# Reordered weight sums, late rows and bank products in the feed-forward part of an attention block

## The chip, the cores and the metric

The kernel runs on one core of a Trainium2 chip. A core has five engines with a queue each: TensorE (PE in the profile, its weight loads PEld) multiplies into PSUM banks of 128 x 512 float32; VectorE (DVE), ScalarE (ACT) and GpSimd (POOL) work element by element; SyncE (SP) only issues transfers here. They wait for one another through semaphores. The metric is the device time in microseconds; lower is better.

## The reference

One layer of an encoder on x of 2048 rows by 1024 columns, in float32. Two kinds of attention come first, then the part this change is about:

```python
h = h + jnp.einsum('bse,ed->bsd', mix, w_out[l])
u2 = rms_norm(h, norm2_w[l])
gate = jnp.einsum('bsd,df->bsf', u2, w_gate[l])
up = jnp.einsum('bsd,df->bsf', u2, w_up[l])
h = h + jnp.einsum('bsf,fd->bsd', jax.nn.silu(gate) * up, w_down[l])
```

The inner width is 2816.

## The kernel before

The attention stages run up to about 1380 us and are untouched by the change. The feed-forward part then works through 22 steps: two halves of 1024 rows, and in each half 11 groups of 256 inner columns. The steps are numbered i = 0 to 21.

**Precision and products.** TensorE multiplies in float16. Each float32 operand is split in a high and a low float16 part, and a product is the sum of three matmuls (high x high, low x high, high x low). Every 2 x 2 block product is done with seven block products in place of eight (Winograd's form of Strassen's scheme), so operands exist as seven combinations `o`.

**A step.** `gate` and `up` each call `quad`, which issues seven products of 12 matmuls each (`product`, L1004), 84 matmuls in all, and adds the parts up on VectorE. The banks are named `pa`, `pm` and `pd`: `pa` and `pd` each take two products, the second added on top of the first after another engine has read the first (L1014 reads `pa`, L1031 reads `pd`). The order of the products in `quad` is pa, pm, pm, pa again, pd, pm, pd again. A finished block goes to a callback `c11`: for gate a SiLU on ScalarE (L1049), for up the multiplication with the gate (L1069) and the split of the result into the buffer `act` (L1063, L98), of which there are two. `down` (L1104) multiplies `act` by the down weight, for two steps at once: for the first half it runs in steps 2, 4, 6, 8 and 10, and in step 11 for the one group left over, each time between gate and up. Its partial sums are read from and written back to the DRAM buffer `hd` through four tiles `hs`. In step 11 the first half's result goes out. In the second half the odd tiles of `hs` use the weight buffers `stages`, which are then idle.

**Loading weights.** In the first half each step's gate, up and down weight is loaded as float32 by `load_ffn`: a transfer into one of two buffers `stages` (L909, L911), a Square on ScalarE (`sq`, L937 for gate and up, L189 for down), a sum or maximum across the partitions with a few matmuls into the bank `fsc` (L945 for gate and up, L182 in `across` for down), a scale worked out by six short VectorE instructions, and then the split into float16 parts on ScalarE, GpSimd and VectorE (L215, L98, L220) and a store of them to the DRAM buffer `split`. The second half reads `split` and does none of this. `load_ffn` is a generator: `begin` runs it through the load and the Square, `end` runs the rest. `quad` calls a hook after its fourth product: in gate `begin` for the next step's gate weight; in up `end` for this step's down weight and then `begin` for the next step's up weight. The other calls stand between the quads.

**Late rows.** The last four of the 16 row tiles get their second norm, transposes and seven combinations inside steps 0 and 1 (`build_x`, another generator, moved on by `tick`; transposes on TensorE at L1178). It occupies one of the two `act` buffers and all four `hs` tiles until it ends. It yields 14 times. Before the change it is moved on in bunches: one step in the gate quad of step 0, three after it, three in the up quad, one after, and all the rest after the gate quad of step 1.

**The order of the work.** The program is traced in the order written, and a scheduler then orders each engine's queue at build time: it plays the program through with estimated durations, and an engine takes, of the instructions that are ready by that estimate, the one traced first. So an instruction can be issued ahead of ones traced before it, and in the built program each queue is fixed. Such an order can be bound by an edge, `tc.issue_after(ins)`: what is traced in its block on `ins`'s engine is queued behind `ins`, without waiting for its end. The kernel before has one, for a transfer.

Of the kernel before, what the change touches and what calls it, by code (L numbers as in the profile page):

```python
# [21 lines left out]
S, D, P = 2048, 1024, 128  # L22
# [18 lines left out]
CU = 3  # L41
# [18 lines left out]
def block(tc, a, out):  # L60
# [3 lines left out]
    with top:  # L64
# [113 lines left out]

        def across(dst, pt, cols):
            k = len(cols)  # L180
            for j, c in enumerate(cols):
                PE.matmul(pt[:, P * j : P * j + P], lhsT=c.to_broadcast([P, P]), rhs=id32[:], start=True, stop=True)  # L182
            DVE.tensor_reduce(dst, pt[:, : P * k], op=ALU.max, axis=AX.X)
# [689 lines left out]
        with ExitStack() as ph2:  # L873
# [20 lines left out]

            rows = []
            stages = fw.tile([P, 2, 2048], F32, name="stages", bufs=1)
            turn = [0]
# [22 lines left out]
            def load_ffn(half, fg, names, W):  # L920
                eng = "ADP" if fg == 0 else WE
                sc = scales.setdefault(fg, {})
                for nme in names:
# [19 lines left out]
                    def columns(m):  # L943
                        for k in range(KT):
                            PE.matmul(pt[:, :256], lhsT=ones[:], rhs=sq[:, 256 * k : 256 * k + 256], start=k == 0, stop=k == KT - 1)  # L945
# [54 lines left out]
            def product(ps_, wv, wo, X, xo, start, stop):  # L1000
                q = 0
                for kt in range(4):
                    for xi, wi in ((0, 0), (1, 0), (0, 1)):
                        PE.matmul(ps_[:].rearrange("p (t n) -> p t n", n=P), lhsT=wv[:, wo, wi, 128 * kt : 128 * kt + 128], rhs=X[xo][:, :, xi, kt, :], start=start and q == 0, stop=stop and q == 11, skip_group_check=not start)  # L1004
                        q += 1

            def quad(wv, X, tag, bufs, c11, hook=None):
                def cst():
                    return fp.tile([P, 512], F32, tag=tag, bufs=bufs, name=nm(tag))

                pa = pst("pa")
                product(pa, wv, 0, X, 0, True, True)
                u2 = cst()
                ACT.copy(u2[:], pa[:])  # L1014
# [16 lines left out]
                DVE.tensor_tensor(c22[:], pd[:], u3[:], ALU.add)  # L1031
# [6 lines left out]
                DVE.tensor_tensor(u2[:], u2[:], pd[:], ALU.add)  # L1038
                c11(0, 1, u2)

            def gate(W, X, hook=None):
                sg = {}

                def on_gate(f, t, c):
                    if (f, t) == (0, 0):
                        s = fp.tile([P, 512], F32, tag="cg", bufs=5, name=nm("cg"))
                    else:
                        s = c
                    ACT.activation(s[:], c[:], AF.Silu, scale=W["kg"][:])  # L1049
                    sg[f, t] = s  # L1050

                quad(W["g"], X, "cg", 5, on_gate, hook)
                note("A", 2000)
                return sg

            def up(W, X, sg, hook=None, final=False):
                if final:
# [25 lines left out]

                quad(W["u"], X, "cu", CU, on_up, hook)
# [12 lines left out]
            def down(half, units, hs, last, hook=None):  # L1097
# [3 lines left out]
                def prod(po, ao, wo, j, start=True):  # L1101
                    for u, (W, act) in enumerate(units):
                        for q, (xi, wi) in enumerate(((0, 0), (0, 1), (1, 0))):
                            PE.matmul(po[:], lhsT=act[:, ao, xi, 128 * j : 128 * j + 128], rhs=W["d"][:, wo, wi, :], start=start and u == 0 and q == 0, stop=u == nu - 1 and q == 2, skip_group_check=not start)  # L1104

# [12 lines left out]
                for j in range(4):  # L1118
                    if j == 2 and hook is not None:
                        hook()  # L1120
                    if j + 1 < 4:
                        hs.append(load_hs(half, j + 1, nu == 3))
                    h0, h1 = hs[j]
# [31 lines left out]
            def build_x():  # L1155
# [11 lines left out]
                for j in (2, 3):  # L1167
# [6 lines left out]
                    for z in (xa, xb):  # L1174
                        for h in range(2):
                            tr = pst("xtr")
                            for k in range(4):
                                PE.transpose(tr[:, P * k : P * k + P], z[:, 512 * h + P * k : 512 * h + P * k + P], id32[:])  # L1178
                            ACT.copy(z[:, 512 * h : 512 * h + 512], tr[:])
                        note("A", 1000)  # L1180
# [3 lines left out]
            W = {}  # L1184
# [35 lines left out]
            for i, (half, fg) in enumerate(steps):  # L1220
# [77 lines left out]
```

## Time and profile before

| | |
|---|---|
| median of 3 runs | 2701.52 us (2700.67 to 2704.35) |
| the profiled execution | 2702.93 us |
| its span | 2701.0 us |
| TensorE busy | 2508.6 us, 93% |
| VectorE busy | 1959.8 us, 73% |
| GpSimd busy | 1517.8 us, 56% |
| ScalarE busy | 1344.7 us, 50% |

In the profile, L1004 is line 1004 of the kernel. A row of a group reads: line, engine, operation, output<-inputs by the program's tile names with buffer numbers left out, shape, count. In the timeline a row starts with its start and its length in us, and ends with the idle time of the engine before it and what ended that. A helper's line stands for all its callers: L98 is any addition or subtraction, L220 any low part of a weight. A tile's name is that of the last user of a buffer, so `pm<-X,wg` can be another of the quad's products. The granted clock is the share of full speed that TensorE was given.

### The profile page before, as it was taken

To read this page: it belongs to the slowest core of one execution; us is meant where nothing else is said; L and a number is where in the kernel's file an instruction comes from. 1 tells how busy PE (TensorE), PEld (TensorE's weight loads), DVE (VectorE), ACT (ScalarE), POOL (GpSimd) and SP (SyncE) were. 2 spreads that over 40 slices of the span, in tenths; PEclk is the share of its full clock that TensorE was granted. 3 is DMA by queue.
4 is the path that set the end of the run, shared out by engine and by line. 5 is a ranking of instruction groups with operands and counts; after the bars stand their busy time and mean duration, and the time that the engine had idled before them with its cause. 6 is when DMAs were issued, how large, how long until landed. Compare 5 with 4: busy or idle time off the path is not lost. (4 is left out here: it accounts for less than half of the span.)

```text
span 2701.0 us, 50505 instructions
## 1 busy us (share of the span) xinstructions
PE 2508.6 (93%) x19628; PEld 1507.6 (56%) x19628; DVE 1959.8 (73%) x3712; ACT 1344.7 (50%) x2487; POOL 1517.8 (56%) x1097
## 2 busy tenths in 40 slices
PE   7998989899988989889999999999999999999999
PEld 4655656577776776567774444444444444444444
DVE  6898879899989889887866877778685543433434
ACT  4665656567978878765634534435352112111121
POOL 2578767768767767545665755665564332322323
PEclk9999999999999999999999999999999999999999
DMA  6778697768989989997996566565748744635532
GB/s 221 211 163 184 143 200 172 172 145 183 195 175 185 178 166 206 208 205 203 230 317 232 211 232 219 207 239 183 253 171 330 304 159 157 234 132 184 202 110 94
DMA packets 619584, 534.40 MB, mean 198 GB/s; under 512 B 480640, under 2 KB 548224, under 8 KB 609104
## 3 DMA queue, kind: packets, MB, share of 16 engines
q1 hardware_dynamic: 617520, 529.09, 70.1%
q8 instruction: 154, 2.52, 0.4%
q0 software_dynamic: 512, 1.36, 0.2%
q14 instruction: 86, 0.70, 0.1%
q10 hardware_dynamic: 1312, 0.72, 0.1%
HBM read 261.08 MB, written 147.32 MB: 151 GB/s over the span
## 5 line engine op out<-in xcount | busy, mean ns | idle before, releaser
L98 POOL TENSOR_TENSOR s<-z,s 128x1024 f16<-128x1024 f32 (+7 forms) x288 | 471.5, 1646 | 141.8 <-ACT s L89 118.2
L506 PE MATMUL sc<-kT,qT 128*128 128x512 f16 (+3 forms) x1520 | 382.7, 354 | 51.1 <-DVE z L622 18.6
L1104 PE MATMUL pd<-wd,act 128*128 128x512 f16 x1764 | 392.8, 380 | 5.3 <-DVE cu L1038 4.7
L621 DVE TENSOR_TENSOR_SCAN z<-z,sc 128x512 f32<-128x512 f32 (+3 forms) x320 | 352.8, 1112 | 56.5 <-ACT sc L619 34.6
L325 PE MATMUL pj<-w,xt 128*128 128x384 f16 x1920 | 354.6, 333 | 17.1 <-ACT raw L374 5.8
L1004 PEld LDWEIGHTS <-wu 128*128 128x128 f16 x1848 | 181.9, 98 | 224.6 <-issue 12.8
L1004 PEld LDWEIGHTS <-wg 128*128 128x128 f16 x1848 | 181.3, 98 | 222.9 <-issue 9.3
L517 PE MATMUL yp<-v,aT 128*128 128x64 f16 (+1 forms) x4896 | 271.2, 205 | 36.9 <-DMA aT<-s 35.7
L517 PEld LDWEIGHTS <-aT 128*128 128x128 f16 x4896 | 239.1, 100 | 114.4 <-DMA aT<-s 46.7
L98 POOL TENSOR_TENSOR act<-cg,act 128x512 f16<-128x512 f32 x109 | 150.7, 1393 | 259.4 <-ACT act L1063 259.4
L1104 PEld LDWEIGHTS <-act 128*128 128x128 f16 x1764 | 172.9, 98 | 213.5 <-issue 7.2
L325 PEld LDWEIGHTS <-xt 128*128 128x128 f16 x1920 | 187.8, 99 | 147.2 <-issue 23.4
L89 ACT CAST s<-z 128x128 f16<-128x128 f32 (+7 forms) x215 | 173.3, 810 | 135.9 <-DMA aT<-s 44.6
L98 POOL TENSOR_TENSOR stages<-stages 128x512 f32<-128x512 f32 x97 | 171.4, 1767 | 116.5 <-DVE wg L220 42.2
L618 ACT ACTIVATE z<-sc,c 128x512 f32<-128x512 f32 (+3 forms) x320 | 211.2, 665 | 24.4 <-PE sc L506 12.4
L98 POOL TENSOR_TENSOR hs<-hs,cu 128x512 f32<-128x512 f32 x102 | 133.6, 1317 | 159.3 <-DVE hs L1110 59.7
L506 PEld LDWEIGHTS <-qT 128*128 128x128 f16 x1520 | 128.8, 99 | 119.7 <-issue 23.9
L831 PE MATMUL po<-wo,mt 128*128 128x256 f16 x1536 | 182.4, 279 | 12.6 <-DVE xf L834 8.6
L1063 ACT CAST act<-cg 128x512 f16<-128x512 f32 x126 | 76.7, 616 | 231.1 <-DVE cg L1069 192.7
L1110 DVE SCALAR_TENSOR_TENSOR hs<-pd,c,hs 128x512 f32<-128x512 f32 x144 | 106.0, 747 | 115.0 <-PE pd L1104 105.3
L341 PE MATMUL pj<-xt,w 128*128 128x128 f16 x2304 | 177.4, 222 | 6.2 <-DVE v L363 5.2
L1004 PE MATMUL pm<-X,wu 128*128 128x512 f16 x792 | 179.8, 381 | 2.1 <-ACT cg L1049 1.7
(254 smaller groups left out, 4812.3 us busy)
## 6 DMA issues: line engine op xcount, KB each, us to landing
xt<-xs SPq DMA_DIRECT2D x112, 512.0 KB, 4.5
hs<-hd SPq DMA_DIRECT2D x72, 512.0 KB, 4.5
hd<-hs SPq DMA_DIRECT2D x56, 512.0 KB, 5.9
split<-wg SPq DMA_DIRECT2D x11, 1792.0 KB, 6.9
split<-wu SPq DMA_DIRECT2D x11, 1792.0 KB, 6.7
split<-wd SPq DMA_DIRECT2D x11, 1792.0 KB, 6.8
wg<-split SPq DMA_DIRECT2D x11, 1792.0 KB, 7.5
wd<-split SPq DMA_DIRECT2D x11, 1792.0 KB, 9.0
```

Source lines behind the costliest of these rows:

```text
L89: ACT.copy(dst, src)
L98: (DVE if e == "D" else POOL).tensor_tensor(dst, a_, b_, op)
L325: PE.matmul(pj[:, :384], lhsT=xv[:, xi, kt, :], rhs=G["w"][:, wi, kt, :], start=n == 0, stop=n == 23)
L341: PE.matmul(o, lhsT=x_ if c == 2 else w_, rhs=w_ if c == 2 else x_, start=n == 0, stop=n == 23)
L506: last = PE.matmul(sc[:, : 128 * w].rearrange("p (t n) -> p t n", n=P), lhsT=G["q"][i // 4][:, a_, i % 4, :], rhs=G["k"][q][:, b_, 0:w, :] ...
L517: PE.matmul(yp[:, y0 : y0 + wd], lhsT=aT[:, a_, :], rhs=v[:, v_ : v_ + wd], start=start and j == 0 and q == 0, stop=stop and j == nb - 1 a ...
L618: ACT.activation(om[:, lo:hi], sc[:, :w], AF.Sigmoid, scale=G["nkz"][:])
L621: DVE.tensor_tensor_scan(ov, ov, sc[:, :w], om[:, hi : hi + 1], op0=ALU.mult, op1=ALU.bypass)
L831: PE.matmul(po[:, sl], lhsT=mt[:, kt, P * xi : P * xi + P], rhs=wos[2 * h + n][wi][:, kt, :], start=q == 0, stop=q == 23)
L1004: PE.matmul(ps_[:].rearrange("p (t n) -> p t n", n=P), lhsT=wv[:, wo, wi, 128 * kt : 128 * kt + 128], rhs=X[xo][:, :, xi, kt, :], start=st ...
L1104: PE.matmul(po[:], lhsT=act[:, ao, xi, 128 * j : 128 * j + 128], rhs=W["d"][:, wo, wi, :], start=start and u == 0 and q == 0, stop=u == nu ...
L1110: DVE.scalar_tensor_tensor(dst, po[:], kd[:], src, op0=ALU.mult, op1=ALU.add)
```

## The change

Five edits:

- `front` keeps the last product's matmul as it is traced, in `product` and in `down`. The sums into `fsc` (for all three weights) and the late rows' transposes get an order edge behind it (`behind`).
- `quad` does pd's first product before pa's second: pa, pm, pm, pd, pa again, pm, pd again. One hook becomes a table of hooks after products 2, 3, 5 and 6; the old hook is the one after the fifth.
- In up's hook the next up weight's `begin` comes before the down weight's `end`.
- The late rows move on by one step per hook: in step 0 one in gate, four in up, one after; in step 1 two in gate, four in up, the rest after up.
- `load_hs` uses `stages` for the odd tiles also where the first half's last sums go out (step 11).

```diff
-        def across(dst, pt, cols):
+        def across(dst, pt, cols, where=None):
             k = len(cols)
-            for j, c in enumerate(cols):
-                PE.matmul(pt[:, P * j : P * j + P], lhsT=c.to_broadcast([P, P]), rhs=id32[:], start=True, stop=True)
+            with where or nullcontext():
+                for j, c in enumerate(cols):
+                    PE.matmul(pt[:, P * j : P * j + P], lhsT=c.to_broadcast([P, P]), rhs=id32[:], start=True, stop=True)
...
+            front = [None]
+
+            def behind():
+                return tc.issue_after(front[0]) if front[0] is not None else nullcontext()
...
-                        for k in range(KT):
-                            PE.matmul(pt[:, :256], lhsT=ones[:], ...)
+                        with behind():
+                            for k in range(KT):
+                                PE.matmul(pt[:, :256], lhsT=ones[:], ...)
...
-                    scale_end((lambda m: across(m, pt, cols)) if nme == "d" else columns, r[:], p[:], True, sW)
+                    scale_end((lambda m: across(m, pt, cols, behind())) if nme == "d" else columns, r[:], p[:], True, sW)
...
-            def quad(wv, X, tag, bufs, c11, hook=None):
+            def quad(wv, X, tag, bufs, c11, hooks):
+                def at(n):
+                    if n in hooks:
+                        hooks[n]()
...
+                at(2)
                 p7 = pst("pm")
                 product(p7, wv, 6, X, 5, True, True)
                 u3 = cst()
                 DVE.tensor_tensor(u3[:], p7[:], u2[:], ALU.add)
-                product(pa, wv, 1, X, 1, False, True)
-                c11(0, 0, pa)
-                note("D", 3000)
-                note("A", 500)
-                if hook is not None:
-                    hook()
+                at(3)
                 pd = pst("pd")
                 product(pd, wv, 2, X, 2, True, True)
                 c22 = cst()
                 DVE.tensor_tensor(c22[:], pd[:], u3[:], ALU.add)
                 c11(1, 1, c22)
+                product(pa, wv, 1, X, 1, False, True)
+                c11(0, 0, pa)
+                note("D", 3000)
+                note("A", 500)
+                at(5)
                 p4 = pst("pm")
                 product(p4, wv, 3, X, 6, True, True)
                 DVE.tensor_tensor(u3[:], u3[:], p4[:], ALU.subtract)
                 c11(1, 0, u3)
+                at(6)
                 product(pd, wv, 5, X, 3, False, True)
...
-            def load_hs(half, j, final=False):
-                if half == 1 and j % 2 and not final:
+            def load_hs(half, j, final=False, last=False):
+                if (half == 1 or last) and j % 2 and not final:
...
-                            for k in range(4):
-                                PE.transpose(tr[:, P * k : P * k + P], ...)
+                            with behind():
+                                for k in range(4):
+                                    PE.transpose(tr[:, P * k : P * k + P], ...)
...
                 def in_gate():
                     begin("g", *steps[i + 1], "g", Wn) if more else None
-                    if i == 0:
+                    if i < 2:
                         tick(1)
...
                 def in_up():
+                    begin("u", *steps[i + 1], "u", Wn) if more else None
                     end("d")
-                    if i == 0:
-                        tick(3)
-                    begin("u", *steps[i + 1], "u", Wn) if more else None
-
-                sg = gate(W, X, in_gate)
-                if i < 2:
-                    tick(3 if i == 0 else 16)
+                    one()
+
+                def one():
+                    if i < 2:
+                        tick(1)
+
+                sg = gate(W, X, {2: one, 5: in_gate} if i == 1 else {5: in_gate})
...
-                act = up(W, X, sg, in_up, not more)
+                act = up(W, X, sg, {2: one, 3: one, 5: in_up, 6: one}, not more)
                 end("u")
-                if i == 0:
-                    tick(1)
+                if i < 2:
+                    tick(16 * i + 1)
```

More of the change, by code (lines that the diff above doesn't have):

```diff
@@ L943, in columns @@
                     def columns(m):
[L944 to L945 removed]
+                        with behind():
+                            for k in range(KT):
+                                PE.matmul(pt[:, :256], lhsT=ones[:], rhs=sq[:, 256 * k : 256 * k + 256], start=k == 0, stop=k == KT - 1)
                         DVE.tensor_reduce(m, pt[:, :256], op=ALU.max, axis=AX.X)
[L948 removed]
+                    scale_end((lambda m: across(m, pt, cols, behind())) if nme == "d" else columns, r[:], p[:], True, sW)
                     sc[nme] = (r, p, sW)
@@ L1003, in product @@
                     for xi, wi in ((0, 0), (1, 0), (0, 1)):
-                        PE.matmul(ps_[:].rearrange("p (t n) -> p t n", n=P), lhsT=wv[:, wo, wi, 128 * kt : 128 * kt + 128], rhs=X[xo][:, :, xi, kt, :], start=start and q == 0, stop=stop and q == 11, skip_group_check=not start)
+                        front[0] = PE.matmul(ps_[:].rearrange("p (t n) -> p t n", n=P), lhsT=wv[:, wo, wi, 128 * kt : 128 * kt + 128], rhs=X[xo][:, :, xi, kt, :], start=start and q == 0, stop=stop and q == 11, skip_group_check=not start).ins
                         q += 1
-            def quad(wv, X, tag, bufs, c11, hook=None):
+            def quad(wv, X, tag, bufs, c11, hooks):
+                def at(n):
+                    if n in hooks:
+                        hooks[n]()
                 def cst():
@@ L1039, in quad, with gate @@
                 c11(0, 1, u2)
-            def gate(W, X, hook=None):
+            def gate(W, X, hooks):
                 sg = {}
@@ L1050, in on_gate, with up @@
                     sg[f, t] = s
-                quad(W["g"], X, "cg", 5, on_gate, hook)
+                quad(W["g"], X, "cg", 5, on_gate, hooks)
                 note("A", 2000)
                 return sg
-            def up(W, X, sg, hook=None, final=False):
+            def up(W, X, sg, hooks, final=False):
                 if final:
@@ L1082, in on_up @@
                     put(6, a12)
-                quad(W["u"], X, "cu", CU, on_up, hook)
+                quad(W["u"], X, "cu", CU, on_up, hooks)
                 note("D", 2440)
                 return act
-            def load_hs(half, j, final=False):
-                if half == 1 and j % 2 and not final:
+            def load_hs(half, j, final=False, last=False):
+                if (half == 1 or last) and j % 2 and not final:
                     h = [stages[:, j // 2, D * q : D * q + D] for q in range(2)]
@@ L1103, in prod @@
                         for q, (xi, wi) in enumerate(((0, 0), (0, 1), (1, 0))):
-                            PE.matmul(po[:], lhsT=act[:, ao, xi, 128 * j : 128 * j + 128], rhs=W["d"][:, wo, wi, :], start=start and u == 0 and q == 0, stop=u == nu - 1 and q == 2, skip_group_check=not start)
+                            front[0] = PE.matmul(po[:], lhsT=act[:, ao, xi, 128 * j : 128 * j + 128], rhs=W["d"][:, wo, wi, :], start=start and u == 0 and q == 0, stop=u == nu - 1 and q == 2, skip_group_check=not start).ins
                 def ust():
@@ L1121, in down @@
                     if j + 1 < 4:
-                        hs.append(load_hs(half, j + 1, nu == 3))
+                        hs.append(load_hs(half, j + 1, nu == 3, last))
                     h0, h1 = hs[j]
```

2 lines of the change are left out of this document (1 added, 1 removed).

## The prediction

> **What bounds the kernel now.** I read the busy table of the page first, then two stretches of the feed-forward part, then the waits of TensorE, then single places in order of time.
>
> ```profile
> PE 2508.6 (93%) x19628; PEld 1507.6 (56%) x19628; DVE 1959.8 (73%) x3712; ACT 1344.7 (50%) x2487; POOL 1517.8 (56%) x1097
> ```
>
> TensorE is the bound, so only time in which it does not multiply can be won. Cut at the first product of the feed-forward part (1425 us) and at the end of its first half:
>
> ```profile
> 1425.00:2110.00 685.00, 649.84 (x3046) 303.18 (x3044) 516.88 (x731) 293.48 (x358) 405.04 (x264) 0.98 0.64 230
> 2110.00:2640.00 530.00, 530.00 (x2457) 240.30 (x2456) 220.97 (x296) 95.92 (x150) 155.86 (x123) 1.00 0.49 176
> ```
>
> The columns are the stretch, its length, the busy time of TensorE, its weight loads, VectorE, ScalarE and GpSimd, and the granted clock. In the second half (2110 on) TensorE is busy for all 530.00 us at full clock: nothing is to be won there. In the first half, which also loads and splits the weights, it idles 685.00 - 649.84 = 35.2 us. What ended that idle time, over the same stretch:
>
> ```profile
> PE fsc L182 <- ACT sq L189: 6.3, 3, 2.3
> PE fsc L945 <- ACT sq L937: 5.9, 4, 2.0
> PE pd L1104 <- DVE cu L1038: 4.7, 2, 2.8
> PE pd L1004 <- DVE cg L1031: 3.6, 4, 1.6
> PE xtr L1178 <- DVE bx L228: 3.4, 2, 3.1
> PE xtr L1178 <- DVE xrs L155: 2.8, 1, 2.8
> PE pa L1004 <- ACT cu L1014: 2.0, 1, 2.0
> PE pa L1004 <- ACT cg L1014: 1.7, 1, 1.7
> PE pm L1004 <- ACT cg L1049: 1.7, 1, 1.7
> PE pd L1004 <- DVE cu L1031: 1.4, 1, 1.4
> ```
>
> Each row has the total, the times and the longest. A second loss follows the longer waits: the clock falls to half. The first two and the last of the seven stretches after 1425 us, each 3.41 us long:
>
> ```profile
> 1448.75:1452.16 3.41, 3.32 (x15) 2.92 (x16) 1.34 (x2) 1.37 (x3) 1.24 (x2) 0.50 0.39 131
> 1493.12:1496.54 3.41, 3.09 (x14) 2.15 (x12) 2.44 (x3) 1.56 (x3) 0.00 (x0) 0.50 0.92 284
> 1994.88:1998.30 3.41, 3.41 (x10) 1.22 (x8) 3.20 (x10) 0.84 (x2) 0.94 (x2) 0.50 0.37 131
> ```
>
> At a granted clock of 0.50 each costs half its length, 1.7 us, which a busy TensorE row hides. All the idle time and seven of these, 35.2 + 7 x 1.7 = 47 us, is the most that any reordering can give.
>
> **The change, part by part.**
>
> (a) *The second bank's two products lie further apart.* A quad is seven products of 12 matmuls. Now pd's first product comes fourth and pa's second comes fifth, so between the two into pd lie two products instead of one, and between the two into pa three instead of two.
>
> ```profile
> 1897.10 2.59 PE pa L1004 x12
> 1783.95 2.75 PE L1004 MATMUL pd<-X,wg 128*128 128x512 f16 x12 [1.62 <-DVE cg L1031]
> ```
>
> A product takes 2.59 us (the chain of waits); the second row is such a wait. One product more is longer than any of the waits on the read of pd (3.6 + 1.4 us) or on the copy of pa (2.0 + 1.7 us), so I take all 8.7 us. The ends are 8.7 and 0: nothing if VectorE, just behind it, is merely late elsewhere. No instruction is added. In the second half the order changes too; TensorE has no idle time there and VectorE is 220.97 of 530.00 us busy, which hides it; I take 0.
>
> (b) *Late rows step by step.* The last four row tiles (their loads, norms, 32 transposes, copies, casts and eight stores) are issued one step per product instead of in bunches, and the transposes get an edge behind the last product traced.
>
> ```profile
> 1448.80 3.75 PE L1178 MATMUL xtr<-id,bx 128*128 128x128 f32 x16 [2.79 <-DVE xrs L155]
> 1492.63 1.48 PE L1178 MATMUL xtr<-id,bx 128*128 128x128 f32 x8 [3.08 <-DVE bx L228]
> ```
>
> Both pairs of transposes stand in a gate quad some two products behind their norm, and wait for it: 3.4 + 2.8 us, and both are followed by half clock (the first two stretches above), 3.4 us. After the change a pair is behind the second product of the up quad: four products, 10.4 us, after the step that traces the norm. I take all 9.6 us, with 0 as the other end.
>
> (c) *Edges for the column sums* (`fsc` L945, for gate and up). Of the four waits two have this shape:
>
> ```profile
> 1616.48 0.60 PE L945 MATMUL fsc<-sq,ones 128*128 128x256 bf16 x4 [1.95 <-ACT sq L937]
> ...
> 1854.33 1.67 PE L1004 MATMUL pa<-X,wu 128*128 128x512 f16 x7
> 1857.96 0.67 PE L945 MATMUL fsc<-sq,ones 128*128 128x256 bf16 x4 [1.96 <-ACT sq L937]
> 1858.43 4.41 PE L1004 MATMUL pd<-X,wg 128*128 128x512 f16 x12
> ```
>
> The sums were put seven matmuls into the next quad, ahead of the gate's last product. The edge puts them behind that product: 12 matmuls instead of 7, or 5 x 0.216 = 1.1 us later (2.59 / 12 = 0.216). That shortens two waits by 2.2 us; the slow matmuls behind the second (12 in 4.41 us) go if its wait falls under a microsecond, 1.7 us. I take 3.9; the ends are 0 and 5.9 + 1.7 = 7.6.
>
> (d) *The down weight's maximum* (`fsc` L182) waits three times, 6.3 us, each time before half clock (in the last row here 12 matmuls take 4.44 us):
>
> ```profile
> 1746.84 2.75 PE L1004 MATMUL pa<-X,wu 128*128 128x512 f16 x12
> 1751.87 0.49 PE L182 MATMUL fsc<-id,m 128*128 128x128 f32 x2 [2.28 <-ACT sq L189]
> 1752.20 4.44 PE L1004 MATMUL pd<-X,wu 128*128 128x512 f16 x12
> ```
>
> It stands behind pa's second product already, so the edge adds nothing here. But its hook moves from behind the fourth product to behind the fifth, 2.59 us, more than the longest wait of 2.28. Against that, the gate's last product no longer slips into this up quad, which makes the quad itself that much earlier against the load. The ends are 0 and 6.3 + 5.1 = 11.4; I take about a third, 4.0, nearer the lower end because the data's time does not move.
>
> (e) *The up load ahead of the down scale.* This moves one 1 MB load on SP, and one Square on ScalarE, ahead of the down weight's two matmuls, its VectorE chain and its four ScalarE products.
>
> ```profile
> 1754.34 0.32 SPq L986 DMA_DIRECT2D split<-wg  x1
> 1754.75 0.39 SPq L911 DMA_DIRECT2D stages<-in_w_up_dram  x1
> ```
>
> The load is already issued 0.41 us after the store that follows the last use of its buffer, so it cannot start sooner: 0. A Square that waits for its load at the head of ScalarE's queue would hold the down weight's products behind it; ScalarE is 293.48 of 685.00 us busy, and that cover takes it. If the cover fails, it costs what a wait on a Square costs in the rows above, at the longest 2.3 us; ends -2.3 and +2.3.
>
> (f) *Load buffers for the last partial sums.* Four of the 512 KB loads of the sums written out at the end of the first half go to the idle weight buffers. That stage (units of one group, just before 2115 us) shows no wait of `pd` on `hs`, since gate products lie between: 0. Without that cover a load's price is the wait it would end:
>
> ```profile
> 2052.84 6.85 PE L1104 MATMUL pd<-wd,act 128*128 128x512 f16 x31 [0.59 <-DVE hs L1110]
> ```
>
> This 0.59 us belongs to the step before, which keeps its buffers. Ends 0 and 0.6.
>
> (g) *What is late next.* The rows hold one of the two `act` buffers and all four `hs` buffers until their last store has read them. Step 1's up quad needs that `act` buffer.
>
> ```profile
> 1498.89 0.23 PE xtr L1178 x2
> ...
> 1514.31 4.97 DMA xcd<-b
> ...
> 1519.39 3.97 DVE wd L220 x2
> 1499.82 2.75 PE L1004 MATMUL pa<-X,wu 128*128 128x512 f16 x12
> 1519.43 1.14 ACT L1063 CAST act<-cg 128x512 f16<-128x512 f32 x2 [0.41 <-ACT wd L215]
> 1531.12 0.59 PE L1104 MATMUL pd<-wd,act 128*128 128x512 f16 x2
> ```
>
> From the last transpose to the landing of the last store it is 1514.31 + 4.97 - 1498.89 = 20.4 us, and `act` is first written at once after that. Now the transposes come behind two products of step 1's up quad instead of ahead of it: 2 x 2.59 + 16 x 0.11 = 7.0 us into it (0.23 / 2 is 0.11 each), against -0.9 (1498.89 against 1499.82). So `act` is written 7.9 us later, and the down products of step 2, which read it 31 us into that quad, can be late by as much; behind `act`, the `cg` buffers come free later and hold up the next gate quad. But the seven casts now run without waiting for their inputs. Ends -7.9 and 0; I take the middle, -4.0.
>
> (h) *VectorE's lateness.* `pd` L1104 waits on L1038, 4.7 us, once before half clock, because VectorE is full there:
>
> ```profile
> 1880.00:1900.00 20.00, 17.17 (x77) 7.85 (x76) 19.81 (x24) 11.53 (x15) 15.19 (x10) 0.91 0.57 192
> ```
>
> It is busy 19.81 of 20 us. The change takes no work from VectorE; I take 0, with 6.4 as the other end.
>
> The sum: 8.7 + 9.6 + 3.9 + 4.0 + 0 + 0 - 4.0 + 0 = 22.2 us. The profiled execution took 2702.93 us, 1.93 around its span of 2701.0, and 1.41 more than the median of 2701.52. So 2702.93 - 22.2 = 2680.7, and against the median 2679.3.
>
> [...]
>
> **Rivals.**
>
> *All waits go* (c, d and h at their upper ends): 8.7 + 9.6 + 7.6 + 11.4 + 6.4 - 4 = 39.7 us, 2661.8. For it: many waits are under one product. Against: a full VectorE and loads that start at the moment their buffer is free.
>
> *The loads take it back.* In a step without a down stage the weights' chain (load, Square, sum, split, next load) runs as long as TensorE's work. If TensorE arrives earlier it only waits longer at the next `fsc`: (a) is returned, (c) and (d) give nothing, and 9.6 - 4.0 = 5.6 us remain, 2695.9. The buffer-bound load at 1754.75 speaks for it; against it, the waits of (a) in steps 0 and 1 lie outside this chain.
>
> *Slower: the up weight becomes late.* The edge puts up's column sum behind all of up's products, and in the steps without a down stage that weight is just ready in time:
>
> ```profile
> 1715.19 1.04 PE L945 MATMUL fsc<-sq,ones 128*128 128x256 bf16 x8
> 1716.71 2.75 PE L1004 MATMUL pd<-X,wu 128*128 128x512 f16 x12
> 1735.20 1.25 PE L1004 MATMUL pm<-X,wu 128*128 128x512 f16 x5 [0.41 <-DVE wu L220]
> ```
>
> Today the sum goes one product ahead of up's last, and up still waits 0.41 us for its weight. A sum later by one product (2.59), the wait of that product itself (1.6) and half clock after it (1.7) would cost 5.9 us in each of five such steps, 29.5: 2679.3 + 29.5 = 2708.8. It decides from 22.2 / 5 = 4.4 us a step. Against: the gate quad that hides the split now follows whole behind the sum, seven products as today.
>
> **How the numbers follow.** The forecast 0.50, its own range 2668 to 2691 (gains of 10 to 33: from (g) in full with (c) and (d) at nothing to (c) and (d) at their upper ends); all waits go 0.15; loads take it back 0.20; up late 0.15. A measurement of this kernel tells about 0.2%, 5.4 us, from no change. Faster takes the first two and 0.09 of the third, whose 5.6 us stand at that bound: 0.74; the same its other 0.11; slower 0.15. The range runs from the first rival, 2660, to 2706, inside the last one.
>
> **What would show it.** (a): no waits of `pa` and `pd` L1004 on L1014 and L1031. (b): `xtr` L1178 waits under 1 us, no half clock in the first two steps. (c), (d): the two `fsc` rows at some 4 and 4 us instead of 5.9 and 6.3, with fewer stretches at 0.50. (g): TensorE waiting near step 2's first down products for `act` or `cg`, some 4 us. The prediction is wrong if `wu` L220 heads TensorE's waits, if the `fsc` rows grow by what the `pd` rows lose, or if idle time appears after 2110 us.

## The result and the profile after

The changed kernel took 2694.54 us (median; 2692.62 to 2698.70), the kernel before 2701.10 in the same session. The ratio is 0.9978, 95% interval 0.9968 to 0.9989: 0.22% or 6.6 us faster. The forecast was 22.2 us.

The profiled execution took 2693.58 us, 1.78 around its span of 2691.8. That is 9.2 us less span than before, but 5.75 of it lie ahead of the feed-forward part, which starts at 1419.44 us instead of 1425.19. TensorE's order there is the same in both kernels, and in the two turns of the banks below that start varies as well, 1420.70 us in one trace and 1425.05 in the other. So stretches of the feed-forward part are compared, not spans.

The edits add 7 lines above `fsc` (L945 is now L952) and 7 above the products (L1004 is L1011, the read of `pd` L1031 is L1038, the copy of `pa` L1014 is L1025); the down weight's maximum L182 is L183, `pd` L1104 is L1117, `xtr` L1178 is L1192.

The table cuts the first half at TensorE's first matmul on the up weight of step 2, 4, 6, 8, 10 and 11. I call the four cycles of two steps A, B, C and D. All in us, from one trace each:

| | gate of step 0 to up of 2 | A | B | C | D | to up of 11 | sum |
|---|---|---|---|---|---|---|---|
| before | 149.48 | 123.47 | 120.13 | 121.19 | 120.06 | 55.26 | 689.59 |
| after | 152.29 | 123.47 | 117.65 | 121.70 | 115.47 | 55.26 | 685.84 |

Before, the windows view of these stretches (start:end, length, then busy time and count of TensorE, its weight loads, VectorE, ScalarE, GpSimd, then granted clock, DMA share, GB/s):

```profile
1425.19:1574.67 149.48, 138.33 (x661) 67.07 (x659) 119.18 (x168) 75.70 (x95) 96.57 (x61) 0.98 0.62 225
1574.67:1698.14 123.47, 115.31 (x542) 53.36 (x541) 95.20 (x134) 52.18 (x62) 74.39 (x49) 0.99 0.62 215
...
1939.46:2059.52 120.06, 114.44 (x533) 52.60 (x532) 84.01 (x118) 46.75 (x57) 64.22 (x44) 0.99 0.62 220
```

After:

```profile
1419.44:1571.73 152.29, 139.57 (x661) 65.92 (x658) 118.57 (x166) 75.61 (x95) 99.53 (x65) 0.96 0.64 227
1571.73:1695.20 123.47, 116.18 (x541) 53.81 (x540) 94.13 (x133) 52.92 (x62) 72.06 (x48) 0.97 0.60 209
1695.20:1812.85 117.65, 113.79 (x541) 52.89 (x540) 91.13 (x132) 52.72 (x62) 71.88 (x49) 1.00 0.61 214
1812.85:1934.55 121.70, 115.55 (x542) 53.69 (x540) 93.19 (x133) 52.59 (x62) 74.14 (x49) 0.97 0.62 217
1934.55:2050.02 115.47, 113.02 (x533) 52.02 (x532) 85.24 (x120) 47.10 (x57) 65.76 (x45) 1.00 0.64 228
```

The first stretch, where the late rows lie, got 2.8 us longer. Cycles B and D got 2.5 and 4.6 us shorter and run at full clock; A and C, with the same work, did not gain and run at 0.97. The three traces with the changed kernel's steps 0 to 2 (this one and the two turns of the banks below) have a first stretch of 151.2 to 152.3 us, the two of the kernel before (with and without such a turn) 148.4 and 149.5, and D is 115.46 to 115.49 in the five whose order there is the same; so I take differences of 2 us and more as real. The first stretch now has two spells of half clock of 6.83 us each, where before it had two of 3.41. After 2105 us TensorE is busy 530.00 of 530.00 us, as before. From up of 11 to TensorE's last matmul another 0.65 us is won (580.59 against 581.24).

What TensorE waits for in the first half, after:

```profile
PE fsc L952 <- ACT sq L943: 11.8, 4, 5.7
PE pd L1011 <- DVE cg L1038: 7.5, 8, 3.3
PE pd L1011 <- DVE xrs L155: 5.2, 1, 5.2
PE pa L1011 <- ACT cg L1025: 1.7, 1, 1.7
PE fsc L183 <- ACT sq L190: 1.6, 2, 1.2
PE pd L1117 <- ACT act L1076: 1.1, 1, 1.1
```

The transposes (`xtr`) are gone from it and the maximum (`fsc` L183) has fallen from 6.3 to 1.6 us. The column sums (`fsc` L952) have doubled from 5.9 to 11.8, and there is a new wait of 5.2 us on VectorE. The two largest waits on the sums lie in cycles A and C, the one on `xrs` in step 1. In cycle A, the timeline of TensorE, then of the DMA queue and of ScalarE:

```profile
1632.60 2.75 PE L1011 MATMUL pm<-X,wg 128*128 128x512 f16 x12
1635.18 1.46 PE L1117 MATMUL pd<-wd,act 128*128 128x512 f16 x6
1641.53 1.86 PE L952 MATMUL fsc<-sq,ones 128*128 128x256 bf16 x8 [4.88 <-ACT sq L943]
1643.18 4.68 PE L1011 MATMUL pa<-X,wg 128*128 128x512 f16 x12
```

```profile
1629.97 0.39 SPq L917 DMA_DIRECT2D stages<-in_w_up_dram  x1
...
1639.58 1.90 ACT L943 ACTIVATE sq<-stages 128x2048 bf16<-128x2048 f32 x1
```

The up weight's load is issued at 1629.97 and its Square starts at 1639.58. The sum of that Square stands in TensorE's queue ahead of `pa`, the gate's first product, and holds it up for 4.88 us; then 12 matmuls take 4.68 us instead of 2.75 because the clock is at half (0.50 from 1640.26 to 1647.09 us). Cycle C has the same row with 5.75 us. That weight is first multiplied only some 50 us later.

In step 1, TensorE's and then VectorE's timeline:

```profile
1474.66 2.75 PE L1011 MATMUL pm<-X,wg 128*128 128x512 f16 x12
1482.61 4.73 PE L1011 MATMUL pd<-X,wg 128*128 128x512 f16 x12 [5.20 <-DVE xrs L155]
```

```profile
1476.31 1.49 DVE L221 SCALAR_TENSOR_TENSOR wu<-stages,c,wu 128x1024 f16<-128x1024 f32 x1 [1.07 <-ACT wu L216]
1477.72 0.68 DVE L1033 TENSOR_TENSOR cg<-pm,cg 128x512 f32<-128x512 f32 x1
1478.32 1.91 DVE L221 SCALAR_TENSOR_TENSOR wu<-stages,c,wu 128x1024 f16<-128x1024 f32 x1
1480.15 1.75 DVE L221 SCALAR_TENSOR_TENSOR wu<-sx,c,wu 128x512 f16<-128x512 f32 x1
1481.82 0.14 DVE L155 TENSOR_SCALAR xrs<-xss 128x1 f32<-128x1 f32 x1
1481.88 0.68 DVE L1038 TENSOR_TENSOR cg<-pd,cg 128x512 f32<-128x512 f32 x1
```

The second product into `pd` waits for the read of the first (L1038). The first had ended by about 1472.1, two products before, but the read stands in VectorE's queue behind three low parts of the up weight and the late row's `xrs`. In step 2 there are three more waits, at the place where (g) looked for them:

```profile
1527.11 0.60 PE L1117 MATMUL pd<-wd,act 128*128 128x512 f16 x2 [1.12 <-ACT act L1076]
1528.40 1.04 PE L1117 MATMUL pd<-wd,act 128*128 128x512 f16 x4 [0.69 <-POOL act L98]
1532.72 5.27 PE L1011 MATMUL pd<-X,wg 128*128 128x512 f16 x12 [3.29 <-DVE cg L1038]
```

The first two go back to the late rows' last store, and the third at least in part: ScalarE stands idle for that store before its first write of `act`, and VectorE, whose read of `pd` ends the third wait, stands idle for ScalarE:

```profile
1525.92 1.66 ACT L1076 CAST act<-cg 128x512 f16<-128x512 f32 x3 [5.94 <-DMA xcd<-b]
1526.57 0.69 DVE L98 TENSOR_TENSOR act<-cg,act 128x512 f16<-128x512 f32 x1 [2.51 <-ACT act L1076]
```

### The profile page after: what moved, and what is told of

It is laid out like the page before. It is cut to its first block, busy times and chain, and to the rows that moved or that the text cites. A ratio compares the mean times of both kernels' runs of the same rounds, so it can differ in the third digit from the quotient of the medians.

```text
span 2691.8 us, 50532 instructions
## 1 busy us (share of the span) xinstructions
PE 2498.3 (93%) x19628; PEld 1500.8 (56%) x19628; DVE 1961.2 (73%) x3710; ACT 1344.5 (50%) x2487; POOL 1516.1 (56%) x1099
## 5 line engine op out<-in xcount | busy, mean ns | idle before, releaser
L1117 PE MATMUL pd<-wd,act 128*128 128x512 f16 x1764 | 391.4, 379 | 3.8 <-ACT act L1076 1.1
L1011 PEld LDWEIGHTS <-wg 128*128 128x128 f16 x1848 | 182.8, 99 | 237.4 <-issue 27.2
L1011 PEld LDWEIGHTS <-wu 128*128 128x128 f16 x1848 | 180.7, 98 | 215.1 <-DVE wu L221 1.8
L1117 PEld LDWEIGHTS <-act 128*128 128x128 f16 x1764 | 172.4, 98 | 212.6 <-issue 3.4
L1123 DVE SCALAR_TENSOR_TENSOR hs<-pd,c,hs 128x512 f32<-128x512 f32 x136 | 100.6, 748 | 110.4 <-PE pd L1117 108.8
L1011 PE MATMUL pm<-X,wu 128*128 128x512 f16 x792 | 179.6, 379 | 0.8 <-DVE wu L221 0.8
```

The costliest lines, as they stand in the source:

```text
L1011: front[0] = PE.matmul(ps_[:].rearrange("p (t n) -> p t n", n=P), lhsT=wv[:, wo, wi, 128 * kt : 128 * kt + 128], rhs=X[xo][:, :, xi, kt, : ...
L1117: front[0] = PE.matmul(po[:], lhsT=act[:, ao, xi, 128 * j : 128 * j + 128], rhs=W["d"][:, wo, wi, :], start=start and u == 0 and q == 0, s ...
L1123: DVE.scalar_tensor_tensor(dst, po[:], kd[:], src, op0=ALU.mult, op1=ALU.add)
```

## The experiments

Unless said otherwise the edit is against the changed kernel, and ratios are to the kernel before, measured in the same session.

**Undoing one part.** The first four ask whether the rows step by step cost time (theory A) or not (B), and whether the sum's place in the queue (C) or the weights' chain itself (D) sets the length of cycles A and C.

*Rows bunched again.*

```diff
-                sg = gate(W, X, {2: one, 5: in_gate} if i == 1 else {5: in_gate})
+                sg = gate(W, X, {5: in_gate})
+                if i < 2:
+                    tick(3 if i == 0 else 16)
...
-                act = up(W, X, sg, {2: one, 3: one, 5: in_up, 6: one}, not more)
+                act = up(W, X, sg, {5: in_up}, not more)
```

> The changed kernel with the late rows moved on in bunches as before (all else of the change stays, the transposes' edge too). Theory A, the rows step by step cost time: their casts, subtractions and stores now compete with step 1's gate and up on VectorE and hold the act buffer longer (TensorE waits of 5.2 us in step 1's gate quad and 5.1 us ahead of and within step 2's first down products, each followed by half clock). Undone, the stretch from the first gate product to step 3's first up product goes from 152.3 us to about 146 (before: 149.5, less 3.4 us of waits on pa and pd), the whole 5 to 6 us faster than the changed kernel, some 2688. Theory B, those waits come from the new product order or the edges: the stretch stays within 2 us of 152.3 and the time at 2694.

(Its mark is step 2's first up product.) Measured: 2701.44 us, 1.0003 (0.9991 to 1.0015); first stretch 155.46. That is neither A's 146 nor B's 152.3: within this change, stepwise rows save 3.2 us of that stretch against bunched ones, and some 6.8 us by the ratios. They do it although step 1 then waits 5.2 us: bunched, `xtr` waits 2.8 us again and `pd` 3.9 us.

*The two products of the second bank adjacent in the list again*, pa's second ahead of pd's first.

```diff
+                product(pa, wv, 1, X, 1, False, True)
+                c11(0, 0, pa)
                 pd = pst("pd")
                 product(pd, wv, 2, X, 2, True, True)
...
-                product(pa, wv, 1, X, 1, False, True)
-                c11(0, 0, pa)
```

> The changed kernel with pa's second product back ahead of pd's first; hooks, edges and rows stay. If the spacing does what the prediction took it for, 5 to 9 us of waits of pa and pd on L1025 and L1038 come back: 2699 to 2703. If the weights' chain sets the pace of the steps without a down stage, only the waits in steps 0 to 2 come back, some 3 us: 2697, and the cycles of two steps from step 2 on stay within 1 us of 123.5, 117.7, 121.7, 115.5.

Measured: 2700.40 us, 1.0004 (0.9994 to 1.0014), sum of the stretches 692.73: 6.9 us given back in the trace, 7.0 by the ratios. It comes from B (121.25) and D (118.38); A and C change by less than 1.5. The waits for the parts `cg` are longer:

```profile
PE pd L1011 <- DVE cg L1042: 9.1, 6, 4.9
PE pm L1011 <- ACT cg L1062: 4.8, 2, 2.4
```

*No edges.*

```diff
             def behind():
-                return tc.issue_after(front[0]) if front[0] is not None else nullcontext()
+                return nullcontext()
```

> The changed kernel without its order edges on the sums and the transposes. By the prediction's step (c) two waits grow by 1.1 us each and some half clock returns: 2 to 4 us slower than the changed kernel, 2697 to 2699. If the edges only move the same wait from one place to another, as the profile after suggests: 2692 to 2696, with the sums' waits near 13 us as they are.

Measured: 2695.22 us, 0.9985 (0.9974 to 0.9996), sum 684.61. The column sums wait 11.8 us with the edges and without. The edges are worth nothing that can be measured, here or below with other banks.

*The up weight's sum kept back to the next gate quad*, behind its third product, in the odd steps.

```diff
-                end("u")
+                if i % 2 and i < 10:
+                    kept = nxt.pop("u")
+                else:
+                    end("u")
...
+                sg = gate(W, X, {2: one, 3: lambda: finish(late), 5: in_gate} if i == 1 else {3: lambda: finish(late), 5: in_gate})
```

> The changed kernel, with the up weight's sum and split for steps 2, 4, 6, 8 and 10 (those with a down stage) traced after the third product of that step's gate quad, not ahead of the quad. Theory C, TensorE loses 4.9 and 5.7 us (and half clock after, 2.7 us) because the sum stands in its queue ahead of work that could go on, while the weight is not needed for another 50 us: the two waits go, and the time falls by up to 15 us, to some 2680. Theory D, the weights' chain sets the pace: TensorE only arrives earlier at the next sum and waits there, less than 4 us gained, 2691 or more.

Measured: 2691.60 us, 0.9972 (0.9964 to 0.9981), sum 682.10. A fell to 118.82, but C stayed (121.67) and B grew to 118.99. The wait on the Square fell to 2.5 us, and others came for it:

```profile
PE pd L1011 <- DVE cg L1038: 8.4, 8, 2.8
PE pd L1117 <- ACT cu L1143: 5.2, 4, 2.5
PE pd L1011 <- DVE xrs L155: 5.2, 1, 5.2
PE pd L1011 <- DVE c L205: 5.0, 1, 5.0
PE fsc L952 <- ACT sq L943: 2.5, 3, 1.3
```

L205 belongs to the scale that follows the sum. The time is where theory D put it (under 4 us gained), but A lost 4.7 us with the same loads, so its length was not that of the weights' chain; the sum's place alone does not free cycle C.

*The up load behind the down scale again.*

```diff
-                    begin("u", *steps[i + 1], "u", Wn) if more else None
                     end("d")
+                    begin("u", *steps[i + 1], "u", Wn) if more else None
```

> The changed kernel with the next up weight's load and Square traced behind the down weight's scale again. The prediction's step (e) put this part at nothing: the time stays at 2694 (2692 to 2697), the cycles of two steps within 1 us. If the Square, now ahead of the down weight's products on ScalarE, is what made steps 0 and 1 longer (152.3 us from the first gate product to step 2's up quad, against 149.5 before), that stretch falls to 149 or below and the time to some 2691.

Measured: 2694.24 us, 0.9982 (0.9969 to 0.9994), sum 686.48. No difference to the changed kernel.

**Why A and C and not B and D.** `pst` hands out the PSUM banks: every fourth tile comes from one pool of banks, the other three from another.

```python
        def pst(t):
            pst_n[0] += 1
            if pst_n[0] % 4:
```

A cycle of two steps takes 13 + 13 + 20 = 46 tiles, and 46 mod 4 is 2, so two neighbouring cycles hand their tiles out in two ways, by turns. In A and C, the order shown above has a `pm` product and six down matmuls first, then the sum, then `pa`, so it looks as if the bank of `pa` was not free yet when the order was made; which tile held it, no view here shows. Theory E says that this makes the bad cycles; the next two kernels change only the counter, and neither add nor drop an instruction.

```diff
                     hs = [load_hs(dh, 0)]
+                if i in (3, 5, 7, 9):
+                    pst_n[0] += 2
```

> The changed kernel, with the rotation of the PSUM banks turned by two places at the start of steps 3, 5, 7 and 9, so that every cycle of two steps gets the bank assignment that the cycles of steps 5-6 and 9-10 have. Theory E: 46 tiles a cycle, taken from a pool of two and a pool of six at a fixed rotation of four, put step 4's and step 8's first gate product on a bank that is not free, so the scheduler fills the place with the up weight's sum, which then waits 4.9 and 5.8 us for its Square. With the other assignment all four cycles take what the good ones take, 115.5 to 118 us; those of 123.5 and 121.7 lose 4 to 6 us each: about 10 us faster than the changed kernel, 2683 to 2686. Theory D (the weights' chain sets the pace): the cycles' lengths stay within 1.5 us of what they are, 2694.

Measured: 2682.67 us, 0.9944 (0.9928 to 0.9960): 11.9 us below the changed kernel's median, and in the traces cycles A to D are 9.5 us shorter. The windows of A to D:

```profile
1576.22:1694.95 118.73, 113.95 (x541) 52.83 (x540) 93.54 (x134) 52.62 (x62) 72.50 (x48) 1.00 0.64 221
1694.95:1812.56 117.61, 113.79 (x541) 52.84 (x540) 91.36 (x132) 52.70 (x62) 72.02 (x49) 1.00 0.62 216
1812.56:1929.53 116.97, 113.64 (x541) 52.85 (x540) 90.99 (x133) 52.91 (x62) 71.98 (x49) 1.00 0.63 221
1929.53:2045.01 115.48, 113.03 (x533) 52.08 (x532) 85.23 (x120) 47.10 (x57) 66.34 (x45) 1.00 0.65 230
```

At the place of the 4.88 us wait, its timeline now reads:

```profile
1637.21 2.75 PE L1011 MATMUL pa<-X,wg 128*128 128x512 f16 x12
1639.80 5.34 PE L1011 MATMUL pm<-X,wg 128*128 128x512 f16 x24
1644.98 2.10 PE L1011 MATMUL pa<-X,wg 128*128 128x512 f16 x9
1646.93 1.04 PE L952 MATMUL fsc<-sq,ones 128*128 128x256 bf16 x8
```

`pa` stands first, the sum almost four products later, and nothing waits. The total of `fsc` L952 is 0.5 us. The opposite, with the counter moved in steps 5, 7 and 9:

> The same turn, but so that every cycle gets the assignment of the cycles of steps 3-4 and 7-8. Theory E: all four cycles take 121.5 to 123.5 us, with a wait of some 5 us at the up weight's sum in each: about 10 us slower than the changed kernel, 2703 to 2706. Theory D: no change, 2694.

Measured: 2705.36 us, 1.0033 (1.0021 to 1.0044), cycles 123.56, 122.85, 123.14, 121.49; its largest wait:

```profile
PE fsc L952 <- ACT sq L943: 23.2, 7, 5.8
```

Now all four cycles are bad, and with the same five edits the kernel is slower than before. The range from the one counter to the other, 22.7 us, is as large as the whole forecast.

*The bank turn in the kernel before, and with no edges.*

> The kernel before with nothing but the same turn of the banks at steps 3, 5, 7 and 9. If the turn alone is the gain, its cycles come down to 115.5 to 118 us and the time to some 2688. If it works only with pd's products two apart, whose waits still end the cycles here: cycles near the 120 us of its better ones, at most 5 us gained in all, 2696 to 2700.

> The kernel with all cycles on the good bank assignment, without the order edges. If the edges are worth nothing, as in the changed kernel: 2680 to 2684, the stretch of steps 0 and 1 1 to 2 us shorter, the cycles within 1 us of 118.7, 117.6, 117.0, 115.5. If the good assignment needs them (a sum that slips ahead of a quad's last product waits there): 2686 or more.

In the kernel before it does nothing: 2700.94 us, 1.0002 (0.9990 to 1.0015), cycles 124.07, 121.93, 121.28, 119.95. With the change but without the edges, the gain is there in full: 2683.35 us, 0.9940 (0.9922 to 0.9959). So the turn needs another of the edits to be worth anything, and the edges are not that one. I did not try it with each of the others. B and D rest on the spacing of (a) (the run with adjacent products) and on the later hook (the last run below), so these two are the likely ones.

**The late rows.** Rows step by step and the transposes' edge, on the kernel before:

```diff
+                            with behind():
+                              for k in range(4):
...
-                sg = gate(W, X, in_gate)
-                if i < 2:
-                    tick(3 if i == 0 else 16)
+                def one():
+                    if i < 2:
+                        tick(1)
+
+                sg = gate(W, X, {2: one, 5: in_gate} if i == 1 else {5: in_gate})
...
+                act = up(W, X, sg, {2: one, 3: one, 5: in_up, 6: one}, not more)
```

> The kernel before with only the late rows moved on step by step and an edge on their transposes alone; products, sums and loads as before. By the prediction's steps (b) and (g) the waits of 6.2 us and 3.4 us of half clock go and 4 us come back at the act buffer: some 5.6 us faster than before, 2694, and the stretch from the first gate product to step 2's up quad 144 us instead of 149.5. If the crowding on VectorE and the act buffer take all of it, as in the profile after: that stretch at 149 to 153 us and the time at 2699 to 2703.

Measured: 2704.19 us, 1.0023 (1.0011 to 1.0034), slower; the first stretch 158.90, 9.4 us more than before. The same read of `pd`, in the same gate quad:

```profile
1486.16 4.37 PE L1009 MATMUL pd<-X,wg 128*128 128x512 f16 x12 [8.03 <-DVE cg L1041]
```

Of two explanations for the waits after, F says that VectorE is too full in steps 1 and 2, G that the rows hold the buffer `act` longer. The rows' subtractions moved to GpSimd, on the kernel with all good cycles:

```diff
-                    yield from x_ops([d2(z) for z in (xa, xb)], d2(xt), 1, j, bufs, "AP", "DP")
+                    yield from x_ops([d2(z) for z in (xa, xb)], d2(xt), 1, j, bufs, "AP", "P")
```

> The kernel with all cycles on the good bank assignment (2682.7 us), and the late rows' subtractions all on GpSimd instead of shared between VectorE and GpSimd. Theory F: a full VectorE (10.0 of 10 us busy at 1465 to 1475 in the profile after) makes the read of pd late in step 1's gate quad, 5.2 us, and half clock follows. Then that wait shrinks and the stretch from the first gate product to step 2's up quad falls from 151.2 us by 4 to 8. Theory G: the act buffer, held until the rows' last store, decides: GpSimd takes longer for them, the store comes later, and the stretch grows, 153 us or more.

Measured: 2683.45 us, 0.9947 (0.9927 to 0.9967); the first stretch 148.96 instead of 151.17. This decides for neither. The large wait, which was to shrink by F, stayed:

```profile
1483.53 4.31 PE L1011 MATMUL pd<-X,wg 128*128 128x512 f16 x12 [5.50 <-DVE xrs L155]
```

And the rows' last store, which was to come later by G, came sooner: `act` is first written 104.1 us after the first gate product instead of 106.5, and ScalarE waits 0.44 us for the store instead of 5.97.

```profile
1524.18 1.66 ACT L1076 CAST act<-cg 128x512 f16<-128x512 f32 x3 [0.44 <-DMA xcd<-b]
```

The three waits of step 2 fall from 4.5 to 3.2 us. That is what a buffer that comes free sooner would do; how much of it the emptier VectorE did, this run does not tell. As for the large wait, the rows' own subtractions do not hold up that read. Three low parts of the weight (1.27, 1.90 and 1.75 us) and the step's own splits stand ahead of it in VectorE's queue; that these are the cause is read from the order, and no run moves them. Cycles A to D take back 2.1 us, so the kernel as a whole is no faster. That the rows get a buffer of their own, which would test G directly, was not tried.

**The hook after the fourth product**, as before the change.

```diff
+                at(5)
                 product(pa, wv, 1, X, 1, False, True)
...
-                at(5)
```

> The changed kernel with the main hook (down weight's maximum, the next loads' begin) back behind the fourth product, now between pd's first and pa's second. By the prediction's step (d) the waits at the down weight's maximum (1.6 us in the profile after, 6.3 before) and their half clock come back: some 4 us slower than the changed kernel, 2698 to 2700. If the later hook is what keeps steps 0 and 1 at 152.3 us, 3 us above before although their waits on pa and pd are fewer: that stretch at 149 or below, and 2691.

Measured: 2692.79 us, 0.9977 (0.9965 to 0.9988), first stretch 150.48, cycles 119.25, 120.77, 119.99, 119.28. The later hook is worth nothing as a whole:

```profile
PE pd L1011 <- DVE cg L1038: 18.1, 9, 3.4
PE pd L1011 <- DVE xrs L155: 5.3, 1, 5.3
PE fsc L952 <- ACT sq L943: 3.9, 3, 1.9
```

With the early hook TensorE waits 10.6 us more for VectorE's read of `pd` and 7.9 us less for the column sums. The wait at the down weight's maximum (`fsc` L183) does not come back: there is no such row at all. The cycles are alike, but none is good.

## Why the prediction was wrong

The sign was right, the size was not: 6.6 us of 22.2. The step that failed is how (b), (c) and (d) were reckoned: the waits of the old trace were priced at their old places, as if the rest of each queue stayed, but the whole order was built anew. In the traces, steps 0 to 2 were to win 9.0 us (9.6 of (b), -4.0 of (g), 3.4 of (a)) and lost 2.8; cycles A to D were to win the other 13.2 and won 6.6, because the new order gave A and C a wait of some 5 us each. With the banks dealt out the other way the same cycles win 16.1, so the banks account for that half of the miss. By its own steps:

- **(a), 8.7 us: right in kind, a little large.** Undoing it gives back some 7 us. The gain lies in B and D only. What was to show it did not: of the waits between the products of a bank (8.7 us) the two of step 1 and step 2 alone, 5.2 and 3.29, make as much again, for VectorE's read can be late by more than two products. The first wait on the copy of `pa`, 1.7 us, stayed as it was.
- **(b), 9.6 us, and (g), -4.0: the sum of the two was wrong.** The transposes no longer wait. But (b) took the end of their wait for a gain and did not ask what VectorE does instead: the read of `pd` now waits 5.2 us in the same gate quad, with half clock behind it (12 matmuls in 4.73 us). The stretch got 2.8 us longer instead of shorter. Against bunched rows in the same kernel the steps save 3.2 us of it, alone on the kernel before they cost 9.4. (g) had the right mechanism and too small a size. The transposes end 7.1 us into the up quad, where 7.0 were reckoned, but from there `act` is first written some 31 us later, not 20.4, so it comes 18 us later into that quad than before, not 7.9. TensorE waits 1.12 + 0.69 + 3.29 = 5.1 us in step 2, and 12 matmuls at half clock then take 5.27 us instead of 2.75: 7.6 us in all, near (g)'s far end. Which of the edits make the first stretch longer than before stays open: none of those undone alone brings 149.48 back (rows 155.46, products 151.97, edges 150.46, load 151.44, hook 150.48).
- **(c), 3.9 us: the step that failed in kind.** The edges do nothing that can be measured, with either bank order. It reckoned the new place of each sum by hand from the trace of before, as if the rest of the order stayed; in A and C the sum went to a place where it waits 4.88 and 5.75 us. An edge only says what the sum is behind, not that it is late enough.
- **(d), 4.0 us: the wait went, but not through the hook, and the time did not.** It fell from 6.3 to 1.6 us, by 4.7 where 4.0 were forecast. With the hook moved back it is gone altogether, so something else in the change ended it, which is open; and the kernel is as fast that way (0.9977 and 0.9978), as other waits stand in its place.
- **(e) and (f), 0: right.** 2694.24 with the load put back; the stretch to the up of step 11 is 55.26 us, as before.
- **(h), 0: not tested.** The wait it left standing, 4.7 us of `pd` on VectorE, is no longer among TensorE's waits, but no run prices that. VectorE stayed full where (b) ran into it, 10.00 of 10 us at 1465 to 1475.
- **Missing: the banks.** With the counter that makes every cycle good, the change is worth 0.56%, 16.1 us by the medians (the kernel before took 2698.76 beside it); with the other it is 0.33% slower. No term held this: the forecast supposed that equal cycles gain alike.

Of the rivals, the loads taking it back came nearest in number (2695.9) but not in mechanism: a cycle without a wait on the chain is possible with the same loads, as the good cycles show. The late up weight did not happen (`wu` L221: 0.8 us). Its opposite did: the sum that was to come too late for its weight came too early for TensorE. All waits going (2661.8) did not happen either, and 2682.67 is the best seen.

On the clock, the wait of 3.29 us in step 2, with the waits of 1.12 and 0.69 us just ahead of it, was followed by half clock:

```profile
1532.70:1536.00 3.30, 3.28 (x8) 1.13 (x8) 2.25 (x2) 3.30 (x5) 2.07 (x3) 0.50 0.38 119
```

So were waits of 2.28 and 1.96 us in the trace before: the granted clock is 0.50 there from 1752.54 and from 1858.35 us, for 3.41 us each.

## What to carry to other kernels

In a queue that is built from estimates, a wait in the old trace prices only its own place: after an edit the whole order is new, so ask of each moved instruction both whether it comes too late for its user and whether it comes too early for its input, and look at what the next instruction in the queue is. Where buffers are dealt out in a fixed rotation, count what one cycle of the loop takes against the rotation's length: if it does not divide, equal cycles can differ, and turning the counter is a free edit worth trying in both directions (in the kernel before it did nothing). And compare equal cycles with one another in the trace; a pattern of long and short ones can point to such a cause.

## What the runs showed of the hardware that I had not expected

In the feed-forward part all seven spells of half clock of the trace before lasted 3.41 us, and all four of the trace after 6.83, the two at the waits of 4.88 and 5.75 us among them. TensorE was busy for 5.56 and 4.73 us of these two, and half of that, an estimated 2.8 and 2.4 us, is lost beside the wait itself.

```profile
1640.26:1647.09 6.83, 5.56 (x18) 2.52 (x18) 6.76 (x6) 3.17 (x5) 5.47 (x4) 0.50 0.56 215
1879.19:1886.02 6.83, 4.73 (x16) 2.25 (x16) 6.55 (x6) 5.25 (x7) 6.75 (x5) 0.50 0.00 0
```

And the length of the wait alone did not tell whether half clock followed. Of these two waits before, half clock (0.50) followed the shorter, from 1633.07 us, and full clock the longer, 1.00 from 1616.48 to 1630.00 us:

```profile
1616.48 0.60 PE L945 MATMUL fsc<-sq,ones 128*128 128x256 bf16 x4 [1.95 <-ACT sq L937]
1632.53 0.49 PE L182 MATMUL fsc<-id,m 128*128 128x128 f32 x2 [1.86 <-ACT sq L189]
```

What brings half clock on, no view here shows.

And the same order of TensorE's work in the attention stages ended at times 5.75 us apart (1419.44 and 1425.19 us) in the two executions compared here, nearly what the change is worth, 6.6 us.
